# A list-scheduling planner with bank order, DMA lanes, held loads and repeated rounds, in a two-layer hybrid decoder trunk

## The chip, the cores and the metric

The kernel runs on one core of one Trainium2 chip. The metric is the device time of one execution in microseconds (us), as a median over runs. Five engines work in parallel, each through its own queue of instructions in a fixed order: PE (TensorE, matmuls; PEld is its loading of weights), DVE (VectorE), ACT (ScalarE), POOL (GpSimd) and SP (SyncE, which here only issues DMAs). ACT and POOL issue DMAs as well.

## The reference

A trunk of two pre-norm residual layers over 256 tokens of width 1024 in float32. Each layer makes one projection of the normalised stream, feeds three causal token mixers from it, gates, projects and sums them, and projects once more:

```python
for layer in range(DEPTH):
    h = rms_norm(x, norm_w[layer])
    proj = jnp.einsum('bsd,de->bse', h, w_in[layer])
    ...
    y_a = mamba2_branch(a_xbc, a_z, a_dt, conv_w[layer], ...)
    y_b = sliding_window_branch(b_q, b_k, b_v, b_z, sinks[layer], cos, sin)
    y_c = forgetting_attention_branch(c_q, c_k, c_v, c_f, c_z, f_bias[layer])
    branch = jnp.einsum('bsiw,iwd->bsid', jnp.stack([y_a, y_b, y_c], axis=2), w_proj[layer])
    g = jax.nn.sigmoid(gates.reshape(b, s, N_BRANCH, d) + gate_bias[layer])
    x = x + jnp.einsum('bsd,de->bse', jnp.sum(g * branch, axis=2), w_out[layer])
return rms_norm(x, final_norm_w)
```

The first mixer is a Mamba-2 scan in chunks of 128 tokens (4 groups of 4 heads), the second attention over a window of 128 with 16 query heads, 4 key heads and a learned sink per head, the third attention with a cumulative forgetting bias. Each has a SiLU gate of its own.

## The kernel before, in words

All weights stream from HBM once, in tiles of 512 KB (`raw`, six buffers), issued by SP. Float32 products are made of three reduced ones: ACT rounds a weight tile to `hi` (fp32r), DVE takes the rest as `lo`, and PE adds hi x high, hi x low and lo x high of the activations. The 256 tokens are two row blocks of 128. Products go to PSUM in two groups of banks: `mm` (three, for the dense products) and `mx` (five, for scores, transposes and scans). Activations live in tiles named by size (`L8`, `L4`, `L2`, `L1`).

The program is not written in the order in which it runs. The functions of `hybrid_trunk` (line 473) call a Recorder, which notes every operation with the tiles it reads and writes; `access` (line 235) finds from these what each operation depends on, by the elements it touches. The order on PE is the source's order, in which small generators (a quad of attention heads, a group of the scan) come up between the dense products after delays in us, the constants `D_...`. `D_CUM` is the delay of the cumulative sum of the log forget gates (`decay_logits`, line 1188).

The order of all other engines is made by a planner. `order_of` (line 267) gives every PE operation a nominal time, works back through the dependences to a due time for every other operation (`deadlines`, 306), and then runs the recorded program through a model (`run`, 322): at each step the engine that can begin first takes the operation with the earliest due time, unless one that is due sooner would be made late by more than `SLIP`. A DMA's landing is modelled with one `wire` that all queues share. The result feeds the next round, four in all; the last one is emitted (`emit`, 455, the emitting line 468, under which the profile lists every instruction).

The places that matter below: `attn_quad` and `swa_quad` (1008, 1161), which make a quad of four heads' scores in four `mx` banks, first narrow matmuls for one token block and then wide ones for the next, take masked maxima on DVE (`nm`, which starts from the negated sink `nsink`), exponentials on ACT (`pp`) and transpose these on PE; `ssd_group` (1277), the scan; `out_end` (1627), which adds the residual to the last projection, squares and sums it, multiplies it by the final norm's weight and by the row's factor `rs`, and stores it; and `load_final` (1683), a broadcast load of `final_norm_w` on ACT's queue.

Before, a load that depends on nothing is planned as soon as its buffer is free and the queue's turn comes.

Of the kernel before, what the change touches and what calls it, by code (L numbers as in the profile page):

```python
# [2 lines left out]

# [46 lines left out]
ENG = mybir.EngineType  # L50
ENGINES = ("tensor", "vector", "scalar", "gpsimd", "sync")
FIRST_WRITES = ("out", "accum_out")
SLIP, OPENING = 0.05, 16.0


class Buf:

    def __init__(self, tag, shape, dtype, space):
        self.tag, self.shape, self.dtype, self.space = tag, list(shape), dtype, space
        self.on_p = space != "dram"  # L60
        free = shape[1:] if self.on_p else shape
        self.n = int(np.prod(free)) if len(free) else 1
        self.ap = None
        self.turn = None
        self.users, self.open, self.last = [], 0, 0.0
# [70 lines left out]
class Op:  # L136

    def __init__(self, i, engine, name, args, kw):
        self.i, self.engine, self.name, self.args, self.kw = i, engine, name, args, kw
        self.ins = self  # L140
        self.deps, self.behind, self.after, self.bufs = set(), set(), [], []
        views = [("out" if k == 0 else "", a) for k, a in enumerate(args)] + list(kw.items())
        views = [(k, a) for k, a in views if isinstance(a, View)]
        self.writes = [a for k, a in views if k in FIRST_WRITES]
        self.reads = [a for k, a in views if k not in FIRST_WRITES]
        if name == "copy_predicated" or kw.get("accum_op") is not None:
            self.reads += self.writes
        sizes = [a.free_size() for _, a in views] or [1]
        self.cap = 1e9
# [48 lines left out]
class Recorder:  # L198
# [36 lines left out]
    def access(self, op, v, writes):  # L235
        b = v.buf
        if not b.users and b not in op.bufs:
            b.turn = self.turns[b.tag] = self.turns.get(b.tag, -1) + 1
            self.bufs.append(b)
            op.bufs.append(b)  # L240
        elif b not in op.bufs:
            op.behind.add(b.users[0].i)
        b.users.append(op)
        q = slice(v.p[0] // 32, (v.p[1] + 31) // 32) if b.on_p else slice(0, 1)
        e = np.unique(v.fx)
        deps = np.unique(b.writer[q][:, e])
        op.deps.update(int(d) for d in deps if d >= 0)
        if not writes:
            if op.engine == "tensor":
                b.pe_reader[q, e] = op.i  # L250
            else:
                mask = np.zeros(b.n, bool)
                mask[e] = True
                b.readers.append((op, q, mask))
            return
        op.deps.update(int(d) for d in np.unique(b.pe_reader[q][:, e]) if d >= 0)
        for r, rq, mask in b.readers:
            if r is not op and rq.start < q.stop and q.start < rq.stop and mask[e].any():
                op.deps.add(r.i)
        b.writer[q, e] = op.i  # L260
# [3 lines left out]
    return op.land if op.dma else op.end + op.lag  # L264


def order_of(rec, bufs_of, rounds=4, verbose=False):
# [12 lines left out]
    before = {}  # L280
    for tag, bs in by_tag.items():
        n = bufs_of[tag]
        for a, b in zip(bs, bs[n:]):
            before[id(b)] = a
    t = 0.0
    for op in ops:
        if op.engine == "tensor":
            op.nominal = t
            t += op.busy
    end = t  # L290
    for _ in range(rounds):
        deadlines(ops, before, end)
        end, before = run(ops, by_tag, bufs_of)
        t = 0.0
        for op in ops:
            if op.engine == "tensor":
                t = op.start if op.start < OPENING else t
                op.nominal = t
                t += op.busy
        end = t + 8.0  # L300
        if verbose:
            print("end", round(end, 1))
    return sorted(ops, key=lambda op: (op.start, op.i))


def deadlines(ops, before, end):
    for op in ops:
        op.late = op.nominal + op.busy if op.engine == "tensor" else min(op.cap, end + 50.0)
    for op in reversed(ops):
        op.due = min(op.nominal, op.late - op.busy) if op.engine == "tensor" else op.late - op.busy  # L310
        for d in op.deps:
            o = ops[d]
            o.late = min(o.late, op.due - (o.away if o.dma else o.lag))
        for b in op.bufs:
            a = before.get(id(b))
            if a is not None:
                for o in a.users:
                    if o.i < op.i:
                        o.late = min(o.late, op.due - (o.away if o.dma else o.lag))


def run(ops, by_tag, bufs_of):
# [8 lines left out]
    waits = {tag: set(range(len(bs))) for tag, bs in by_tag.items()}  # L331
    soon = {e: sorted((op for op in ops if op.engine == e), key=lambda op: (op.due, op.i)) for e in ENGINES[1:]}
    before = {}
# [4 lines left out]
    wire = 0.0  # L338
    done = 0
    forced = False  # L340

# [10 lines left out]

    def when(op):
        t = op.ready
        for b in op.bufs:
            p = place_time(b)
            if p is None:
                return None
            skipped = sum(x < b.turn for x in waits[b.tag])
# [31 lines left out]
    while done < len(ops):  # L391
        best = None
        for e in ENGINES:
            if e == "tensor":
                if at == len(pe) or pe[at].left:
                    continue
                c = [(when(pe[at]), pe[at])]
            else:
                c = [(when(op), op) for op in queues[e]]
            c = [(max(r, free[e]), op) for r, op in c if r is not None]  # L400
# [3 lines left out]
            r, op = min(((r, op) for r, op in c if r <= t0 + 1e-9), key=lambda x: (x[1].due, x[1].i))  # L404
            if e != "tensor" and not forced and t0 > OPENING:
                until = guarded(e, t0, op)
                if until is not None:
                    c = [(r, op) for r, op in c if r + op.busy <= until + 0.02 or op.due < until]
# [3 lines left out]
                    r, op = min(((r, op) for r, op in c if r <= t0 + 1e-9), key=lambda x: (x[1].due, x[1].i))  # L412
            if best is None or r < best[0]:
                best = (r, e, op)
        forced = best is None
        if forced:
            continue
# [1 line left out]
        op.start, op.end = r, r + op.busy  # L419
        free[e] = op.end  # L420
        if op.dma:
            if op.start < OPENING:
                wire = max(wire, op.end + 0.8) + op.kb / 330
                op.land = max(wire + 1.0, op.end + 2.2)
            else:
                wire = max(wire, op.end + 0.8) + op.kb * (1.5 if op.kb < 270 else 1.0) / 270
                op.land = max(wire + 2.0, op.end + (4.3 if e == "gpsimd" else 2.8))
        for b in op.bufs:
            _, i = place_time(b)
            old = places[b.tag][i][1]  # L430
            if old is not None:
                before[id(b)] = old
            places[b.tag][i] = (None, b)
            waits[b.tag].discard(b.turn)
            b.slot = i
        if e == "tensor":
            at += 1
# [8 lines left out]
        for o, whole in op.after:  # L446
            o.left -= 1
            o.ready = max(o.ready, f if whole else op.start + 0.01)
            if not o.left and o.engine != "tensor":
                queues[o.engine].append(o)  # L450
        done += 1
# [1566 lines left out]
```

## Time and profile before

| | |
|---|---|
| median of 3 runs | 820.79 us (820.53 to 822.17) |
| profiled execution, its own time | 822.48 us |
| its span in the trace | 820.8 us |
| mean granted TensorE clock | 0.996 |
| instructions | 14838 |
| HBM read over the span | 154.71 MB, 191 GB/s |

Times in the views are us from the start of the span. A row of the timeline gives the start, the duration of the group, the engine, the line, the operation, the tile written and those read, the shape, the count, and in brackets the idle time of the engine before it with what ended that. Since every instruction has line 468, tiles tell the places apart: `mx<-L,qt` are scores of a sliding-window quad, `mm<-hi,L` and `mm<-L,hi` dense products. The durations of neighbours overlap, as engines begin an instruction before the last has drained.

### The profile page before, as it was taken

What the parts mean: (1) busy time and instruction counts of PE and PEld (TensorE: products, weight loads), DVE (VectorE), ACT (ScalarE), POOL (GpSimd) and SP (SyncE); (2) the same over time, 40 slices, a digit from 0 to 9 for tenths busy, and PEclk for the clock granted to TensorE, in tenths of its full rate; (3) what the DMA queues carried; (4) which work ended last, traced back from release to release, by engine and by line L of the source; (5) the groups of instructions that cost most, each with busy time, mean ns of one, the idle gap of its engine ahead of it and who ended that gap; (6) DMA issues with size and microseconds to landing.
All of it is one profiled execution on the core that took longest, in us unless ns stands there. A gap on an engine that the chain in (4) does not pass through costs nothing.

```text
span 820.8 us, 14838 instructions
## 1 busy us (share of the span) xinstructions
PE 803.6 (98%) x5160; PEld 714.4 (87%) x5160; DVE 684.9 (83%) x1416; ACT 542.4 (66%) x1146; POOL 165.7 (20%) x236
## 2 busy tenths in 40 slices
PE   7999999999999999999999999999999999999996
PEld 6998888988988988888998898888888888888896
DVE  5968898998889997796685889989888989959874
ACT  5876788775666795544465568777757668755461
POOL 4245312130303300020001731222212120001100
PEclk9999999999999999999999999999999999999999
DMA  9899897797836575666668967789987465556731
GB/s 267 265 282 221 212 245 189 220 269 222 224 113 221 173 216 168 203 222 208 210 226 259 246 157 222 194 216 255 242 255 200 151 197 162 177 198 217 231 103 52
DMA packets 138826, 170.43 MB, mean 208 GB/s; under 512 B 9352, under 2 KB 106464, under 8 KB 138752
## 3 DMA queue, kind: packets, MB, share of 16 engines
q1 hardware_dynamic: 114960, 140.53, 56.5%
q0 software_dynamic: 13328, 13.29, 9.9%
q10 hardware_dynamic: 10464, 15.67, 6.0%
q8 instruction: 41, 0.67, 0.3%
q14 instruction: 33, 0.27, 0.1%
HBM read 154.71 MB, written 2.16 MB: 191 GB/s over the span
## 4 chain that ended last, share of the span: by engine, by line
PE 95%; DVE 2%; DMA 1%; issue 0%; SPq 0%; ACT 0%; DVEq 0%; ACTq 0%
PE mm L468 83%; PE mx L468 12%; DMA raw<-in_w_in_dram 1%; DVE L L468 1%; SPq L468 0%; ACT hi L468 0%; DVE lo L468 0%; DVE pp L468 0%; ACT L L468 0%; DVE sm L468 0%; DVE rs L468 0%; DVEq L468 0%; DVE nm L468 0%; ACTq L468 0%; DVE ss L468 0%
## 5 line engine op out<-in xcount | busy, mean ns | idle before, releaser
L468 DVE TENSOR_TENSOR lo<-raw,hi 128x1024 fp32r<-128x1024 f32 (+2 forms) x292 | 329.7, 1144 | 56.3 <-ACT hi L468 46.7
L468 PE MATMUL mm<-L,hi 128*128 128x512 f32 x1056 | 355.1, 388 | 0.0
L468 ACT ACTIVATE hi<-raw 128x1024 fp32r<-128x1024 f32 (+2 forms) x292 | 281.3, 975 | 99.2 <-PE mm L468 75.4
L468 PE MATMUL mm<-hi,L 128*128 128x512 f32 (+2 forms) x1168 | 303.4, 349 | 1.5 <-ACT L L468 1.2
L468 PE MATMUL mm<-L,lo 128*128 128x256 f32 x1056 | 267.1, 273 | 0.0
L468 PEld LDWEIGHTS mm<-hi,L 128*128 128x128 f32 x1168 | 206.0, 190 | 24.7 <-issue 1.8
L468 PEld LDWEIGHTS mm<-L,hi 128*128 128x128 f32 x1056 | 195.5, 190 | 26.6 <-issue 3.0
L468 PEld LDWEIGHTS mm<-L,lo 128*128 128x128 f32 x1056 | 202.8, 192 | 5.5
L468 PE MATMUL mm<-lo,L 128*128 128x512 f32 (+2 forms) x584 | 201.2, 347 | 0.0
L468 ACT ACTIVATE L<-L 128x256 f32<-128x256 f32 (+2 forms) x184 | 89.4, 505 | 68.7 <-DVE L L468 62.5
L468 PEld LDWEIGHTS mm<-lo,L 128*128 128x128 f32 x584 | 110.3, 190 | 10.7
L468 POOL DMA_DIRECT2D L<-L x80 | 65.2, 859 | 206.8 <-ACT L L468 166.6
L468 ACT ACTIVATE L<-mm 128x256 f32<-128x256 f32 (+2 forms) x202 | 67.9, 373 | 44.3 <-PE mm L468 37.4
L468 ACT ACTIVATE pp<-pp,nm 128x128 f32<-128x128 f32 (+1 forms) x96 | 40.8, 427 | 26.9 <-DVE nm L468 26.7
L468 DVE TENSOR_TENSOR L<-mm,L 128x256 f32<-128x256 f32 (+1 forms) x70 | 37.1, 532 | 22.5 <-PE mm L468 22.1
L468 DVE SCALAR_TENSOR_TENSOR L<-L,vec,L 128x255 f32<-128x255 f32 (+3 forms) x112 | 51.2, 476 | 1.3 <-ACT L L468 0.9
L468 POOL TENSOR_SCALAR_AFFINE_SELECT bias<-bias 128x128 f32<-128x128 f32 x64 | 32.6, 558 | 74.4 <-DMA bias<-cumd 74.0
L468 DVE SCALAR_TENSOR_TENSOR L<-L,L 128x256 f32<-128x256 f32 (+1 forms) x94 | 44.2, 479 | 1.0 <-ACT L L468 0.8
L468 ACT ACTIVATE L<-mx 128x512 f32<-128x512 f32 (+3 forms) x48 | 26.5, 572 | 13.8 <-PE mx L468 13.8
L468 DVE TENSOR_TENSOR L<-L,L 128x512 fp32r<-128x512 f32 (+2 forms) x56 | 32.6, 595 | 0.3
L468 POOL TENSOR_TENSOR sm<-sm,mhalf 128x8 f32<-128x8 f32 (+2 forms) x5 | 6.1, 1222 | 129.3 <-DVE sm L468 129.3
L468 POOL TENSOR_TENSOR L<-L,L 128x512 f32<-128x512 f32 (+1 forms) x12 | 15.6, 1330 | 77.4 <-DVE L L468 77.4
(139 smaller groups left out, 678.2 us busy)
## 6 DMA issues: line engine op xcount, KB each, us to landing
raw<-in_w_in_dram SPq DMA_DIRECT2D x191, 512.0 KB, 5.0
raw<-in_w_proj_dram SPq DMA_DIRECT2D x48, 512.0 KB, 5.1
L<-L POOLq DMA_DIRECT2D x72, 128.0 KB, 5.1
raw<-in_w_out_dram SPq DMA_DIRECT2D x16, 512.0 KB, 5.2
bias<-cumd ACTq DMA_DIRECT2D x16, 256.0 KB, 4.6
L<-cumd ACTq DMA_DIRECT2D x8, 512.0 KB, 6.6
L<-in_gate_bias_dram ACTq DMA_DIRECT2D x12, 256.0 KB, 4.1
qt<-L POOLq DMA_DIRECT2D x16, 128.0 KB, 5.2
```

Source lines behind the costliest of these rows:

```text
L468: getattr(getattr(nc, op.engine), op.name)(*map(real, op.args), **{k: real(v) for k, v in op.kw.items()})
```

## The change

Five edits, all in the planner but the last.

1. The Recorder's `access` keeps a table `latest` per PSUM buffer: an access by one engine depends on the latest accesses of every other engine to the same buffer, whatever elements they touch. Accesses of different engines to a bank thus stand in the source's order.
2. The model of DMAs has eight lanes for the queues of SP and ACT and eight for POOL's: a DMA begins when the eighth last before it has landed. Each queue has a wire, and they slow each other.
3. A load that depends on nothing, is no weight tile and is due after 10 us is held behind the PE operation that nominally begins `LEAD` = 20 us before its due time.
4. Seven rounds in place of four; from the third on a PE operation that came late is given an earlier due time in the next, and the round with the earliest end is kept. `SLIP` is 0.3 instead of 0.05.
5. `D_CUM` is 20 instead of 17.

```diff
-D_GN1, D_GN2, D_CUM, D_H, D_M = 8.0, 3.0, 17.0, (4.8, 6.4), 5.0
+D_GN1, D_GN2, D_CUM, D_H, D_M = 8.0, 3.0, 20.0, (4.8, 6.4), 5.0
...
-SLIP, OPENING = 0.05, 16.0
+SLIP, OPENING, LEAD = 0.3, 16.0, 20.0
...
         b.users.append(op)
+        if b.space == "psum":
+            for e, o in b.latest.items():
+                if e != op.engine:
+                    op.deps.update(o)
+            if op.engine == "tensor":
+                b.latest[op.engine] = [op.i]
+            else:
+                b.latest.setdefault(op.engine, []).append(op.i)
...
+            for op in ops:
+                if op.dma and not op.deps and op.bufs and op.bufs[0].tag != "raw" and op.due > 10.0:
+                    x = pe[bisect.bisect(at, op.due - LEAD) - 1]
+                    op.behind.append(x.i)
+                    op.held = True
+                    x.after.append((op, False))
+        end, before = run(ops, by_tag, bufs_of)
+        t = late = last = 0.0
+        for op in pe:
+            gap, last = op.start - last, op.end
+            if op.start > OPENING and gap > 0.03:
+                late += gap
+                if n > 1:
+                    op.early += gap + 0.3
...
+        if best is None or end < best[0]:
+            best = (end, [(op.start, op.end) for op in ops], [b.slot for b in rec.bufs])
...
     def when(op):
         t = op.ready
+        if op.dma:
+            t = max(t, lanes[op.engine == "gpsimd"][-8])
...
-                wire = max(wire, op.end + 0.8) + op.kb * (1.5 if op.kb < 270 else 1.0) / 270
-                op.land = max(wire + 2.0, op.end + (4.3 if e == "gpsimd" else 2.8))
+            early = op.start < OPENING
+            now, c = op.end + 0.8, op.kb / (330 if early else 300)
+            left = max(wire[q] - now for q in wire if q != e)
+            wire[e] = max(wire[e], now) + c + max(0.0, min(c, left))
```

The order on PE is the same but for the cumulative sums, on SP the same. In a row below, a name is the tile's tag with its buffer and its number, and the brackets name the engines or DMA lanes whose semaphores the instruction waits for.

PE, the wide score matmuls of layer 0's first quad (`mx` 10 to 13 are its four banks, `qt` the queries), before:

```order
L468 MATMUL mx_3_12_946<-L8_5_5_759,qt_0_0_844 128x256
L468 MATMUL mx_0_13_948<-L8_5_5_759,qt_0_0_844 128x256
L468 MATMUL mx_2_10_942<-L8_5_5_759,qt_0_0_844 128x256 [waits DVE_49]
L468 MATMUL mx_4_11_944<-L8_5_5_759,qt_0_0_844 128x256 [waits DVE_49]
L468 MATMUL mx_3_12_946<-L8_5_5_759,qt_0_0_844 128x256 [waits DVE_49]
L468 MATMUL mx_0_13_948<-L8_5_5_759,qt_0_0_844 128x256
```

The same place now:

```order
L511 MATMUL mx_3_12_922<-L8_5_5_702,qt_0_0_775 128x256
L511 MATMUL mx_0_13_924<-L8_5_5_702,qt_0_0_775 128x256
L511 MATMUL mx_2_10_918<-L8_5_5_702,qt_0_0_775 128x256
L511 MATMUL mx_4_11_920<-L8_5_5_702,qt_0_0_775 128x256
L511 MATMUL mx_3_12_922<-L8_5_5_702,qt_0_0_775 128x256
L511 MATMUL mx_0_13_924<-L8_5_5_702,qt_0_0_775 128x256
```

The second four matmuls no longer wait for DVE: the instructions and their order are unchanged.

ACT in the opening (`hi` and `raw` 0 to 3 are the first weight tiles, `L2` 4 and 10 the two halves of a gate's bias), before:

```order
L468 DMA L2_0_4_79<-in_gate_bias_dram 128x512
L468 ACT_TABLE_LOAD
L468 ACTIVATE tab_0_0_67<-tab_0_0_67 128x1 [waits DVE_49]
L468 ACTIVATE L2_1_0_111,ss_0_0_112<-L8_0_0_69 128x512 [waits DMAHW1_49]
L468 ACTIVATE L2_2_1_131,ss_0_0_112<-L8_0_0_69 128x512 [waits DMAHW3_49]
L468 ACTIVATE L8_2_2_141<-L8_1_1_125 128x512 [waits DVE_49]
L468 DMA L2_3_10_149<-in_gate_bias_dram 128x512 [waits DMAHW4_49]
L468 ACTIVATE hi_0_0_159<-raw_0_0_83 128x512
L468 ACTIVATE L8_2_2_141<-L8_1_1_125 128x512 [waits DVE_49]
L468 ACTIVATE hi_0_0_159<-raw_0_0_83 128x512 [waits DMAHW5_49]
```

and now:

```order
L511 ACTIVATE hi_1_1_175<-raw_1_1_100 128x512 [waits DMAHW5_49]
L511 ACTIVATE hi_1_1_175<-raw_1_1_100 128x512
L511 ACTIVATE L2_2_2_192,ss_0_0_120<-L8_0_0_69 128x512 [waits DMAHW6_49]
L511 ACTIVATE L2_3_3_202,ss_0_0_120<-L8_0_0_69 128x512
L511 ACTIVATE L8_2_2_142<-L8_1_1_129 128x512 [waits DVE_49]
L511 ACTIVATE hi_2_2_219<-raw_2_2_112 128x512 [waits DMAHW0_49]
L511 ACTIVATE L8_2_2_142<-L8_1_1_129 128x512 [waits DVE_49]
L511 ACTIVATE hi_2_2_219<-raw_2_2_112 128x512
L511 ACTIVATE hi_3_3_239<-raw_3_3_126 128x512 [waits DMAHW1_49]
L511 ACTIVATE hi_3_3_239<-raw_3_3_126 128x512
L511 DMA L2_4_4_257<-in_gate_bias_dram 128x512 [waits DMAHW7_49]
L511 ACTIVATE hi_4_4_264<-raw_4_4_131 128x1024 [waits DMAHW2_49]
```

The first bias load has gone behind the rounding of weight tile 3 and the second to the stretch around 131 us; the per-head loads on POOL's queue go behind PE operations in the same way.

ACT in the tail (`L8` 35 holds the residual of both row blocks, `ss` their sums of squares, `rs` the rows' factors; `L4` 27 is the final norm's weight), before:

```order
L468 ACTIVATE L2_1_104_9621,ss_3_3_9622<-L8_5_35_9615 128x256 [waits DVE_49]
L468 ACTIVATE L2_8_105_9628,ss_0_4_9629<-L8_5_35_9615 128x256 [waits DVE_49,Pool_49]
L468 ACTIVATE L2_5_107_9660,ss_3_3_9622<-L8_5_35_9615 128x512 [waits DVE_49]
L468 ACTIVATE sm_2_14_9694<-sm_1_13_9669 128x1 [waits DVE_49]
L468 ACTIVATE L8_5_35_9615<-L8_5_35_9615,rs_1_5_9704 128x384 [waits DVE_49]
L468 DMA out_0_dram<-L8_5_35_9615 128x384 [waits Activation_49]
L468 ACTIVATE L2_2_110_9734,ss_0_4_9629<-L8_5_35_9615 128x512 [waits DVE_49]
L468 ACTIVATE sm_5_18_9760<-sm_0_17_9743 128x1 [waits DVE_49]
L468 ACTIVATE L8_5_35_9615<-L8_5_35_9615,rs_2_6_9766 128x384 [waits DVE_49]
L468 DMA out_0_dram<-L8_5_35_9615 128x384 [waits Activation_49]
```

and now:

```order
L511 ACTIVATE L2_2_107_9655,ss_3_3_9619<-L8_5_35_9612 128x512 [waits DVE_49]
L511 ACT_TABLE_LOAD
L511 ACTIVATE sm_2_14_9687<-sm_1_13_9664 128x1 [waits DVE_49]
L511 ACTIVATE L2_3_110_9723,ss_0_4_9626<-L8_5_35_9612 128x512 [waits DVE_49]
L511 DMA L4_1_27_9743<-in_final_norm_w_dram 128x1024
L511 ACTIVATE sm_5_18_9749<-sm_0_17_9732 128x1 [waits DVE_49]
L511 ACTIVATE tab_0_0_67<-ones_0_0_90 128x1
L511 ACTIVATE L8_5_35_9612<-L8_5_35_9612,rs_1_5_9697 128x384 [waits DVE_49]
L511 ACTIVATE L8_5_35_9612<-L8_5_35_9612,rs_2_6_9755 128x384 [waits DVE_49]
L511 DMA out_0_dram<-L8_5_35_9612 128x384 [waits Activation_49] x2
```

The load of the norm's weight has moved here from some 140 rows further up (there behind gate bias 88), and the two stores stand together at the end. DVE at the same place (`mm` 225 and 226 are the last two products of the second row block), before:

```order
L468 TENSOR_TENSOR L8_5_35_9615<-mm_0_225_9681,L2_0_109_9380 128x512 [waits DMAHW5_49,PE_49]
L468 TENSOR_REDUCE sm_0_17_9743<-ss_0_4_9629 128x1 [waits Activation_49]
L468 SCALAR_TENSOR_TENSOR L8_5_35_9615<-L8_5_35_9615,L4_2_27_8186 128x512 [waits DVE_49]
L468 TENSOR_SCALAR sm_0_17_9743<-sm_0_17_9743 128x1 [waits DVE_49]
L468 TENSOR_TENSOR L8_5_35_9615<-mm_2_226_9723,L1_9_351_8855 128x256 [waits PE_49]
L468 ISA L2_3_111_9756,ss_0_4_9629<-L8_5_35_9615 128x256 [waits DVE_49]
L468 ISA ss_0_4_9629 128x1
L468 SCALAR_TENSOR_TENSOR sm_0_17_9743<-ss_0_4_9629,sm_0_17_9743 128x1 [waits DVE_49]
L468 SCALAR_TENSOR_TENSOR L8_5_35_9615<-L8_5_35_9615,L4_2_27_8186 128x256
L468 RECIPROCAL sm_2_19_9762<-sm_5_18_9760 128x1 [waits Activation_49]
L468 SCALAR_TENSOR_TENSOR sm_1_20_9764<-sm_2_19_9762,sm_0_17_9743 128x1 [waits DVE_49]
L468 SCALAR_TENSOR_TENSOR rs_2_6_9766<-sm_1_20_9764,sm_2_19_9762 128x1 [waits DVE_49]
```

and now:

```order
L511 TENSOR_TENSOR L8_5_35_9612<-mm_2_226_9712,L1_10_351_8852 128x256 [waits PE_49]
L511 ISA L2_4_111_9746,ss_0_4_9626<-L8_5_35_9612 128x256 [waits DVE_49]
L511 ISA ss_0_4_9626 128x1
L511 SCALAR_TENSOR_TENSOR sm_0_17_9732<-ss_0_4_9626,sm_0_17_9732 128x1 [waits DVE_49]
L511 RECIPROCAL sm_2_19_9751<-sm_5_18_9749 128x1 [waits Activation_49]
L511 SCALAR_TENSOR_TENSOR sm_1_20_9753<-sm_2_19_9751,sm_0_17_9732 128x1 [waits DVE_49]
L511 SCALAR_TENSOR_TENSOR rs_2_6_9755<-sm_1_20_9753,sm_2_19_9751 128x1 [waits DVE_49]
L511 SCALAR_TENSOR_TENSOR L8_5_35_9612<-L8_5_35_9612,L4_1_27_9743 128x512 [waits DMAHW2_49]
L511 SCALAR_TENSOR_TENSOR L8_5_35_9612<-L8_5_35_9612,L4_1_27_9743 128x512
L511 SCALAR_TENSOR_TENSOR L8_5_35_9612<-L8_5_35_9612,L4_1_27_9743 128x256 x4
L511 TENSOR_SCALAR L8_5_35_9612<-L8_5_35_9612,rs_1_5_9697 128x640 [waits DVE_49]
L511 TENSOR_SCALAR L8_5_35_9612<-L8_5_35_9612,rs_2_6_9755 128x640 [waits DVE_49]
```

All multiplications by the norm's weight stand behind the second row block's factor, with a wait for the load's lane on the first.

More of the change, by code (lines that the diff above doesn't have):

```diff
@@ L64, in __init__ @@
         self.turn = None
-        self.users, self.open, self.last = [], 0, 0.0
+        self.users, self.open, self.last, self.latest = [], 0, 0.0, {}
         self.writer = np.full((4, self.n), -1, np.int32)
@@ L284, in order_of @@
             before[id(b)] = a
+    pe = [op for op in ops if op.engine == "tensor"]
     t = 0.0
-    for op in ops:
-        if op.engine == "tensor":
+    for op in pe:
+        op.nominal, op.early = t, 0.0
+        t += op.busy
+    end, best = t, None
+    for n in range(rounds):
+        deadlines(ops, before, end)
+        if not n:
+            at = [op.nominal for op in pe]
+            for op in ops:
[6 more added lines that the diff above has]
+        t = late = last = 0.0
+        for op in pe:
+            gap, last = op.start - last, op.end
[3 more added lines that the diff above has]
+                    op.early += gap + 0.3
+            t = op.start if op.start < OPENING else t
             op.nominal = t
             t += op.busy
[L290 to L299, printed above, removed]
+        if best is None or end < best[0]:
+            best = (end, [(op.start, op.end) for op in ops], [b.slot for b in rec.bufs])
+        if verbose:
+            print("round", n, "end", round(end, 2), "late", round(late, 2))
         end = t + 8.0
-        if verbose:
-            print("end", round(end, 1))
+    for op, (op.start, op.end) in zip(ops, best[1]):
+        pass
+    for b, b.slot in zip(rec.bufs, best[2]):
+        pass
     return sorted(ops, key=lambda op: (op.start, op.i))
@@ L309, in deadlines @@
     for op in reversed(ops):
-        op.due = min(op.nominal, op.late - op.busy) if op.engine == "tensor" else op.late - op.busy
+        op.due = op.late - op.busy
+        if op.engine == "tensor":
+            op.due = min(op.nominal, op.due) - op.early
         for d in op.deps:
@@ L330, in run @@
     places = {tag: [(0.0, None)] * bufs_of[tag] for tag in by_tag}
-    waits = {tag: set(range(len(bs))) for tag, bs in by_tag.items()}
+    waits = {tag: list(range(len(bs))) for tag, bs in by_tag.items()}
     soon = {e: sorted((op for op in ops if op.engine == e), key=lambda op: (op.due, op.i)) for e in ENGINES[1:]}
+    for op in ops:
+        if op.held:
+            waits[op.bufs[0].tag].remove(op.bufs[0].turn)
     before = {}
@@ L358, in when @@
                 return None
-            skipped = sum(x < b.turn for x in waits[b.tag])
+            skipped = bisect.bisect_left(waits[b.tag], b.turn)
             if skipped and sum(old is None or not old.open for _, old in places[b.tag]) <= skipped:
@@ L414, in run @@
                 best = (r, e, op)
+        if best is None and forced:
+            raise RuntimeError("no operation can begin")
         forced = best is None
@@ L421, in run @@
         if op.dma:
[L422 to L425, printed above, removed]
-                wire = max(wire, op.end + 0.8) + op.kb * (1.5 if op.kb < 270 else 1.0) / 270
-                op.land = max(wire + 2.0, op.end + (4.3 if e == "gpsimd" else 2.8))
+            early = op.start < OPENING
+            now, c = op.end + 0.8, op.kb / (330 if early else 300)
+            left = max(wire[q] - now for q in wire if q != e)
+            wire[e] = max(wire[e], now) + c + max(0.0, min(c, left))
+            for q in wire:
+                if q != e and wire[q] > now:
+                    wire[q] += min(c, wire[q] - now)
+            op.land = max(wire[e] + (1.0 if early else 2.5),
+                          op.end + (2.2 if early else 4.5 if e == "gpsimd" else 3.2))
+            lanes[e == "gpsimd"].append(op.land)
         for b in op.bufs:
@@ L433, in run @@
             places[b.tag][i] = (None, b)
-            waits[b.tag].discard(b.turn)
+            waits[b.tag].remove(b.turn)
             b.slot = i
@@ L448, in run @@
             o.ready = max(o.ready, f if whole else op.start + 0.01)
+            if not o.left and o.held:
+                bisect.insort(waits[o.bufs[0].tag], o.bufs[0].turn)
             if not o.left and o.engine != "tensor":
```

8 lines of the change are left out of this document (5 added, 3 removed).

## Prediction

> **What bounds the kernel now.** The first part of the page, its busy times, comes first:
>
> ```profile
> PE 803.6 (98%) x5160; PEld 714.4 (87%) x5160; DVE 684.9 (83%) x1416; ACT 542.4 (66%) x1146; POOL 165.7 (20%) x236
> ```
>
> TensorE is busy for 803.6 of 820.8 us, so only 17.2 us are to be had from waiting. The table by stretches says where they lie (columns: stretch, its length, busy time and instructions of PE, PEld, DVE, ACT and POOL, granted clock, DMA share, GB/s):
>
> ```profile
> 0.00:20.00 20.00, 15.36 (x89) 12.74 (x90) 10.64 (x19) 11.42 (x23) 9.59 (x28) 1.00 0.93 264
> 20.00:70.00 50.00, 50.00 (x324) 46.13 (x326) 40.08 (x62) 39.22 (x81) 21.62 (x30) 1.00 0.97 273
> 455.00:480.00 25.00, 23.44 (x152) 20.38 (x151) 18.81 (x40) 14.08 (x33) 14.24 (x19) 0.93 0.92 208
> 800.00:821.00 21.00, 14.47 (x91) 13.15 (x89) 9.55 (x29) 3.73 (x12) 0.00 (x0) 0.91 0.14 51
> ```
>
> 4.6 us are missing in the opening, 6.5 at the end, where TensorE has no more work, and 6.1 between. At 455 to 480 the clock dips too: 7% of 25 us, 1.75 us. The waits of PE name the releasers (us in total, times, longest):
>
> ```profile
> PE mx L468 <- DVE nm L468: 3.7, 6, 1.6
> PE mx L468 <- DVE L L468: 1.3, 3, 0.6
> PE mm L468 <- ACT L L468: 1.2, 1, 1.2
> PE mm L468 <- DVE L L468: 1.1, 2, 0.6
> ```
>
> The first row is the sliding-window quads, the second and fourth mostly the scans, the third the opening. Everywhere else PE runs without a gap, so time goes down only by what goes from these rows, and goes up by what the new order puts before a matmul or behind the last one.
>
> **The quads: 7.6 us less.** A quad is 24 score matmuls, then eight wide ones that write, for the second half, banks which DVE is still reading for the first half's maxima (nm). From PE's timeline stand the narrow part of quad 1, then the wide parts of the quads that wait (of three alike, at 142.82, 498.62 and 545.19, the first and the last), and a quad without a wait:
>
> ```profile
> 69.80 1.16 PE L468 MATMUL mx<-L,qt 32*128 32x128 f32 x24
> 71.39 1.25 PE L468 MATMUL mx<-L,qt 32*128 32x256 f32 x8 [0.43 <-DVE nm L468]
> ...
> 96.52 0.71 PE L468 MATMUL mx<-L,qt 32*128 32x256 f32 x8 [0.43 <-DVE nm L468]
> ...
> 142.82 0.98 PE L468 MATMUL mx<-L,qt 32*128 32x256 f32 x8 [0.43 <-DVE nm L468]
> ...
> 471.87 1.57 PE L468 MATMUL mx<-L,qt 32*128 32x256 f32 x8 [1.56 <-DVE nm L468]
> ...
> 545.19 0.98 PE L468 MATMUL mx<-L,qt 32*128 32x256 f32 x8 [0.43 <-DVE nm L468]
> ```
> ```profile
> 119.65 1.59 PE L468 MATMUL mx<-L,qt 32*128 32x128 f32 x32
> ```
>
> Each waiting quad takes 1.16 + gap + wide part; less the 1.59 of the free one that is 1.25, 0.71, 0.98, 2.70, 0.98 and 0.98: 7.6 us. In the new order the wide matmuls carry no wait for DVE, since DVE's reads now follow the second write. All 7.6 lie on PE, hence on the path. The clock's dip stands around the 1.56 us gap; about 0.45 of its 1.75 us is in that quad's 2.70 already, so 1.3 more go with it if the gap is the cause, nothing if not. I take 1.3.
>
> **The scans: 2.3 us less.** In each layer the last matmuls of two sums wait for DVE, which reads the same bank early:
>
> ```profile
> 233.33 0.32 PE L468 MATMUL mm<-L,L 128*64 128x128 f32 x1 [0.57 <-DVE L L468]
> ...
> 235.45 0.43 PE L468 MATMUL mx<-L,L 128*64 128x128 f32 x2 [0.58 <-DVE L L468]
> ```
>
> That is 1.15 us a layer, 2.3 in two (the two rows of waits on DVE L, 2.4 in all, leave no room for more). D_CUM moves three cumulative-sum matmuls a layer behind the next weight tile; they take the same time there, and what hangs on them (a round trip through DRAM) is not needed for over 10 us: nothing.
>
> **The opening: 2.0 us less.** Both gate-bias loads of layer 0 and the small per-head and conv loads leave the first 18 us. What the queues there carry (packets, MB, share of the 16 engines in 0 to 20 us), and PE's waits there for weights:
>
> ```profile
> q1 hardware_dynamic: 4025, 4.62, 70.8%
> q0 software_dynamic: 416, 0.13, 11.6%
> q10 hardware_dynamic: 304, 0.53, 10.5%
> ```
> ```profile
> 8.76 0.49 PE L468 MATMUL mx<-hi,L 128*128 128x256 f32 x2 [0.38 <-ACT hi L468]
> 9.80 0.94 PE L468 MATMUL mx<-hi,L 128*128 128x256 f32 x6 [0.55 <-ACT hi L468]
> ...
> 17.43 1.30 PE L468 MATMUL mm<-hi,L 128*128 128x256 f32 x6 [1.25 <-ACT L L468]
> ```
>
> 0.66 of 5.28 MB go, 12.5% of 20 us: the weights come up to 2.5 us sooner. But PE's own order, its filler matmuls included, stays; only its gaps can close. From the first weight on these are 0.38 + 0.55 + 1.25 and four small ones, about 2.5. I take 2.0, between 0 and 2.5, nearer the top because the moved bytes alone would allow it.
>
> **New waits: 0.9 us more.** The sinks' load of layer 0 now stands behind a PE operation, so that the first quad's nsink comes on POOL behind two rope transfers, and DVE's nm behind lo 27. By hand, from the before's times of these rows, its probabilities are ready at about the instant at which PE transposes them: 0 to 1.2, say 0.5, and as little again (0.4) for one weight split (lo 139, at 419 us) that gets several operations ahead of it.
>
> **The tail: 4.6 us more.** The load of final_norm_w was issued at 660.8 us. It now stands on ACT behind the last 512-wide square, and DVE's six multiplications by it, which were spread between the last evictions, stand behind everything but the two row scalings. ACT's and DVE's end before:
>
> ```profile
> 812.55 0.63 ACT L468 ACTIVATE L<-L 128x512 f32<-128x512 f32 x1 [3.29 <-DVE L L468]
> 813.09 0.19 ACT L468 ACTIVATION_READ_ACCUMULATOR L<-L 128x1 f32 x1
> ```
> ```profile
> 813.38 0.68 DVE L468 SCALAR_TENSOR_TENSOR L<-L,L 128x512 f32<-128x512 f32 x1
> ...
> 815.51 0.42 DVE L468 SCALAR_TENSOR_TENSOR L<-L,L 128x256 f32<-128x256 f32 x1
> ...
> 816.50 0.55 DVE L468 TENSOR_SCALAR L<-L,rs 128x640 f32<-128x640 f32 x1
> ```
> ```profile
> L<-in_final_norm_w_dram ACTq DMA_DIRECT2D x1, 512.0 KB, 5.5
> bias<-cumd ACTq DMA_DIRECT2D x1, 256.0 KB, 3.3
> ```
> ```profile
> out_dram<-L SPq DMA_DIRECT2D x2, 320.0 KB, 3.2
> ```
>
> In the before's clock the load is issued at 813.3. It took 5.5 us among other traffic; half its size took 3.3, and the other 256 KB at the opening's 264 GB/s are 1.0 more. With nothing else on the queues I take 4.1, with 3.3 and 5.5 as ends: it lands at 817.4, 0.9 after the instant (816.5) at which the last row scaling began. Then six multiplications, 2 x 0.60 + 4 x 0.35 without their overlap, 2.6; then the other row block's scaling, 0.5, before the last one. So the last scaling begins 4.0 us later. Both blocks' results, 1 MB, then leave at once where one left before, whose 320 KB took 3.2 us: 0.6 more (0 to 1.0). Sum 4.6, ends 3.2 and 6.6. No other work hides it, since PE has ended at 814.5.
>
> The Trainium skill, page DMA: Bandwidth & Descriptors, section "Rules for kernel authors", speaks against this edit: issue a DMA early and wait for it late, so that its fixed cost overlaps. The same page ("Anatomy of one DMA") fits 2.0 us plus the bytes at 436 GB/s, by which the load would take an estimated 3.2 us and the tail 3.7 instead of 4.6. The 3.3 and 5.5 above lie over that, and they decide.
>
> **Sum.** 7.6 + 1.3 + 2.3 + 2.0 = 13.2 less, 0.9 + 4.6 = 5.5 more: 7.7 us less than the profiled execution's 822.48, 814.8. The median of the runs shown, 820.79, is 1.7 below that execution: **813.1 us**.
>
> **Rivals.**
> - The tail is hidden: the multiplications fit in DVE's idle time, or the load comes earlier than its place suggests. Against it: its row has only the two scalings behind it, and in the stretch 800 to 821 nothing else remains. 813.1 - 4.6 = 808.5; chance 0.13.
> - The opening gives nothing, because the moved loads return where the DMA engines are 0.97 busy (20 to 70 us) and weights come late there, and the tail costs its upper end: 813.1 + 2.0 + 2.0 = 817.1. For it: that row's 0.97. Against it: PE has no gap in those 50 us, at 273 GB/s. Chance 0.16.
> - Only part of the waits goes, the scans' and the dip staying, with both of these: 817.1 + 3.6 = 820.7, no change; chance 0.07.
> - Slower: the wait goes from the bank to the transposes of the probabilities. DVE reads a quad's scores only after the whole quad, ACT's exponentials stand behind weight splits, and PE meets the transposes too early. Before, the first quad's probabilities were ready 7.9 us ahead of use (75.25 to 83.16); in the new order that reserve is nearly gone there, so it can be.
>
> ```profile
> 74.57 0.68 DVE L468 TENSOR_TENSOR pp<-pp,rsum 128x512 f32<-128x512 f32 x1
> ```
> ```profile
> 83.16 0.60 PE L468 MATMUL mx<-ident,pp 128*128 128x128 f32 x4
> ```
> This rival decides above 1.3 us in each of the eight quads ((822.4 - 813.1 + 0.9) / 8); at 2 us each the time is 813.1 + 16 - 0.9 = 828.2. Against it: at the other quads the rows ahead of the exponentials did not grow so. Chance 0.09.
>
> **How the numbers follow.** The forecast's case has 0.55. Its own bounds: all gains full and the tail cheap (3.2), 809.7; opening nil and tail 6.6, 817.1. The range 809.0 to 818.5 leaves out the fully hidden tail, the no-change and the slower case, and half the chance of those near its edges. A measurement of this kernel tells 0.2%, 1.6 us, from no change: faster 0.84 (0.55 + 0.13 + 0.16), same 0.07, slower 0.09.
>
> **What would show it.** Right: the row PE mx <- DVE nm is gone, a quad takes 1.59 everywhere, the clock is 1.00 at 455 to 480, PE's gap of 1.25 us ahead of 17.43 closes and the row that it stands in comes some 2 us sooner, and in the tail DVE waits for final_norm_w's DMA and ends some 7 us after the last matmul (2.6 before). Wrong: a new wait of PE for pp or hi in the quads, gaps in 20 to 70, or a tail of the old length.

## The result, and the profile after

The changed kernel takes 809.37 us (median of 4 runs, 809.29 to 809.45) where the kernel before took 821.48 beside it (820.53 to 822.72): a ratio of 0.9852, with a 95% interval of 0.9835 to 0.9869. That is 12.1 us faster, and 3.7 under the forecast of 813.1. The profiled execution took 809.29, its span is 807.6, 13.2 less than before.

The page's busy times of the kernel after, then its table by stretches (columns as in the prediction):

```profile
PE 795.6 (99%) x5160; PEld 711.8 (88%) x5160; DVE 683.3 (85%) x1416; ACT 542.3 (67%) x1146; POOL 172.0 (21%) x236
```
```profile
0.00:20.00 20.00, 17.68 (x124) 16.59 (x125) 13.69 (x28) 14.22 (x26) 5.85 (x19) 1.00 0.92 309
20.00:70.00 50.00, 50.00 (x333) 45.57 (x332) 40.67 (x61) 37.40 (x78) 18.88 (x25) 1.00 0.99 265
...
455.00:480.00 25.00, 25.00 (x188) 22.89 (x187) 21.09 (x51) 17.98 (x53) 17.00 (x26) 1.00 0.96 216
785.00:808.00 23.00, 13.30 (x85) 12.13 (x83) 8.60 (x28) 4.35 (x10) 0.00 (x0) 0.90 0.19 69
```

From 20 us to its end PE is full but for 0.3 us, the clock is 1.00 at 455 to 480 where it was 0.93, and in the opening PE has begun 124 matmuls by 20 us where it had begun 89. All waits of PE that are left:

```profile
PE mx L511 <- POOL ident L511: 1.4, 1, 1.4
PE mx L511 <- DMA L<-in_x_dram: 0.7, 1, 0.7
PE mx L511 <- DVE es L511: 0.3, 1, 0.3
```

The waits for `nm`, for the scans' reads and for ACT in the opening are gone; one is new, for `es` (the sinks' term of the row sums), at the transposes of layer 0's first quad. The scores of that quad, and of layer 1's, stand as one row each, as wide as the quad that never waited:

```profile
65.88 1.59 PE L511 MATMUL mx<-L,qt 32*128 32x128 f32 x32
```
```profile
460.72 1.59 PE L511 MATMUL mx<-L,qt 32*128 32x128 f32 x32
```

Laying PE's matmuls of the two traces side by side, in their common order, shows where the lead over before grows. Each row names a place, and gives the start of the matmul just after it in both traces, the lead there, and what the place itself adds to the lead:

| place | before | after | lead | gained here |
|---|---|---|---|---|
| weight tile 3's first `lo` matmul | 18.79 | 14.87 | 3.92 | 3.9 |
| after quad 1, layer 0 | 72.57 | 67.41 | 5.16 | 1.25 |
| at its transposes | 83.16 | 78.48 | 4.68 | -0.5 |
| after quad 2 | 97.16 | 91.80 | 5.36 | 0.72 |
| after quad 4 | 143.73 | 137.39 | 6.34 | 0.98 |
| after the two scans' waits, layer 0 | 235.81 | 227.66 | 8.15 | 1.8 |
| after quad 1, layer 1 | 473.37 | 462.24 | 11.13 | 2.70 |
| 2.7 us later (the dip of the clock) | 476.09 | 463.66 | 12.43 | 1.30 |
| after quad 2 | 499.53 | 486.12 | 13.41 | 0.98 |
| after quad 4 | 546.10 | 531.71 | 14.39 | 0.98 |
| after the scans' waits, layer 1 | 638.18 | 621.98 | 16.19 | 1.8 |

Between these places only a transpose at 393 us adds more, 0.3. At the end PE leads by 16.2 us, and the span by 13.2: the tail gives 3.0 back. It was 6.3 from the last matmul to the span's end and is 9.3. Its rows on DVE and ACT after:

```profile
800.14 0.16 DVE L511 SCALAR_TENSOR_TENSOR rs<-sm,sm 128x1 f32<-128x1 f32 x1
800.22 2.63 DVE L511 SCALAR_TENSOR_TENSOR L<-L,L 128x512 f32<-128x512 f32 x6
802.76 1.01 DVE L511 TENSOR_SCALAR L<-L,rs 128x640 f32<-128x640 f32 x2
```
```profile
796.38 0.63 ACT L511 ACTIVATE L<-L 128x512 f32<-128x512 f32 x1 [4.58 <-DVE L L511]
796.39 0.34 ACTq L511 DMA_DIRECT2D L<-in_final_norm_w_dram  x1
```
```profile
L<-in_final_norm_w_dram ACTq DMA_DIRECT2D x1, 512.0 KB, 3.7
```

The load is issued while ACT still squares (796.39, not after it), takes 3.7 us and lands at 800.1, as the last row factor comes (800.14). So its flight is hidden, and DVE goes from the factor to the multiplications without idle time. What is paid is the multiplications (2.63 us) that now stand in one row behind the factor, and the first row block's scaling.

### The profile page after: what moved, and what is told of

It reads as the page before. It is cut to its first block, busy times and chain, and to the rows that moved or that the text cites. A ratio compares the mean times of both kernels' runs of the same rounds, so it can differ in the third digit from the quotient of the medians.

```text
span 807.6 us, 14854 instructions
## 1 busy us (share of the span) xinstructions
PE 795.6 (99%) x5160; PEld 711.8 (88%) x5160; DVE 683.3 (85%) x1416; ACT 542.3 (67%) x1146; POOL 172.0 (21%) x236
## 4 chain that ended last, share of the span: by engine, by line
PE 96%; POOL 1%; DVE 1%; issue 1%; DMA 0%; ACT 0%; DVEq 0%; POOLq 0%; ACTq 0%
PE mm L511 83%; PE mx L511 13%; POOL L L511 1%; DVE L L511 1%; DMA L<-in_x_dram 0%; POOL hb L511 0%; POOL qt L511 0%; ACT L L511 0%; DVE pp L511 0%; DVE nm L511 0%; DVE es L511 0%; DVE sm L511 0%; DVEq L2057 0%; POOL nsink L511 0%; ACT sm L511 0%
## 5 line engine op out<-in xcount | busy, mean ns | idle before, releaser
L511 POOL DMA_DIRECT2D L<-L x80 | 68.0, 900 | 184.2 <-ACT L L511 176.9
L511 POOL TENSOR_SCALAR_AFFINE_SELECT bias<-bias 128x128 f32<-128x128 f32 x64 | 39.0, 707 | 84.3 <-DMA bias<-cumd 84.0
L511 DVE SCALAR_TENSOR_TENSOR L<-L,vec,L 128x254 f32<-128x254 f32 (+3 forms) x112 | 51.9, 478 | 2.2 <-ACT L L511 2.0
L511 ACT ACTIVATE L<-L,vec 128x256 f32<-128x256 f32 (+1 forms) x48 | 26.8, 566 | 14.2 <-DMA L<-L 14.1
```

Of the source, the lines that this page charges most:

```text
L511: getattr(getattr(nc, op.engine), op.name)(*map(real, op.args), **{k: real(v) for k, v in op.kw.items()})
```

## The experiments

Every run's ratio is against runs of the kernel before on the same chip, whose median there was 822.4 to 822.6. In what follows "lead" is again the lead of PE over the kernel before in the aligned traces.

**Final norm's load free.** The held loads without the one of 512 KB on ACT:

```diff
-                if op.dma and not op.deps and op.bufs and op.bufs[0].tag != "raw" and op.due > 10.0:
+                if op.dma and not op.deps and op.bufs and op.bufs[0].tag != "raw" and op.due > 10.0 and not (op.kb > 500 and op.engine == "scalar"):
```

> The changed kernel, but the load of the final norm's weight alone is not held. Main theory: its late place costs the tail 3.0 us (all six multiplications behind the last row factor), so the time is 809.4 - 3.0 = 806.4, and the stretch from the last matmul to the end is 6.3 us again instead of 9.3. Rival: the tail is set by the last stores and the row factors, and the moved load meets busy queues near 660 us: 809.4 or a little more.

Measured 806.03 (ratio 0.9794, 0.9775 to 0.9814), span 804.3. The multiplications stand between the last evictions again, and the last scaling comes one row behind the last factor:

```profile
799.00 0.42 DVE L511 SCALAR_TENSOR_TENSOR L<-L,L 128x256 f32<-128x256 f32 x1
...
799.80 0.16 DVE L511 SCALAR_TENSOR_TENSOR rs<-sm,sm 128x1 f32<-128x1 f32 x1
800.00 0.56 DVE L511 TENSOR_SCALAR L<-L,rs 128x640 f32<-128x640 f32 x1
```

From the last row factor's start to the last scaling's start it is 0.20 us; in the changed kernel it is 3.1 (800.14 to about 803.2). The late load was a loss of the change, and this version beats both kernels.

**No bank order.** The changed kernel without edit 1:

```diff
-        if b.space == "psum":
-            for e, o in b.latest.items():
-                if e != op.engine:
-                    op.deps.update(o)
-            ...
```

> The changed kernel without the bank order in access; loads held, lanes, rounds and D_CUM as changed. Main theory: the waits of PE on the quads' and scans' banks come back, 7.8 + 3.6 us, and the clock's dip of 1.3 with them: about 822. Rival: the repeated rounds and the larger slip already take half of those waits, and about 815 is seen.

Measured 815.89 (0.9912, 0.9888 to 0.9935): the main theory fails by half. PE's waits of this run:

```profile
PE mx L503 <- DVE nm L503: 1.3, 3, 0.4
PE mx L503 <- DVE L L503: 1.2, 2, 0.6
PE mm L503 <- DVE L L503: 1.2, 2, 0.6
```

The scans' four waits are back, and three of the quads'. Three quads stay free: the first of both layers, so that the gap of 1.56 and the dip stay away, and layer 1's second (why that one does was not traced). Bank order is then worth 815.89 - 809.37 = 6.5 on top of the rest: in the alignment three quads (1.0 each) and the scans (3.6) make 6.5. In this run DVE reads the first quad's first half only after it has waited for the negated sink, some 6 us after PE's second write (67.6):

```profile
73.92 0.35 DVE L503 CUSTOM_DVE_ANT_0 pp<-mx,wmask,nsink 128x128 f32<-128x128 f32 x1 [0.51 <-POOL nsink L503]
```

**Bank order alone**, in the kernel before:

```diff
...
         b.users.append(op)
+        if b.space == "psum":
+            for e, o in b.latest.items():
+                if e != op.engine:
+                    op.deps.update(o)
+            ...
```

> The kernel before with the bank order in access and nothing else of the change. Main theory: quads, scans and the dip give 12.7 us alone, 821.5 - 12.7 = 808.8, the opening and the tail as before. Rival: without the new model of the DMAs and the repeated rounds the later reads make new waits elsewhere, and half is lost: about 815.

Measured 811.66 (0.9859, 0.9833 to 0.9885). Alone it frees all the banks' waits: the lead grows by 12.5 from 20.8 us on, where 12.7 was expected. But the new plan's opening is 2.4 longer, by this wait, with a dip behind it:

```profile
18.24 1.52 PE L476 MATMUL mm<-hi,L 128*128 128x256 f32 x8 [2.54 <-ACT L L476]
```
```profile
20.00:25.00 5.00, 5.00 (x32) 5.00 (x32) 4.33 (x10) 3.76 (x6) 3.31 (x5) 0.67 0.96 344
```

**Nothing held.** The changed kernel without edit 3:

```diff
-                if op.dma and not op.deps and op.bufs and op.bufs[0].tag != "raw" and op.due > 10.0:
+                if False:
```

> The changed kernel with no load held. Main theory: the opening goes back to the old one (+3.9) and the tail as well (-3.0): 810.3, with the gate biases in the first 10 us. Rival: the opening is shorter because of the new order of ACT and the row sums, not of the loads: 806.4.

Measured 822.54 (0.9998, 0.9988 to 1.0007): neither theory. PE falls 10 us behind the kernel before in the first 33 us. The chain of waits shows what was not foreseen:

```profile
3.84 5.43 DMA hb<-in_sinks_dram
9.27 0.09 issue
9.36 0.44 POOL nsink L511
...
10.92 4.99 DMA hb<-in_d_skip_dram
...
16.92 4.91 DMA hb<-in_a_log_dram
21.85 0.21 ACT nega L511
22.07 0.53 ACT hi L511
```

The small per-head loads run one behind the other on POOL, each some 5 us in flight, and the planner has put the ACT operation that uses the last of them (`nega`) ahead of weight tile 2's rounding. ACT's queue, and with it every weight, waits for a load of 8 KB.

**ACT's loads free.** The loads on POOL held, those on ACT not:

```diff
-                if op.dma and not op.deps and op.bufs and op.bufs[0].tag != "raw" and op.due > 10.0:
+                if op.dma and not op.deps and op.bufs and op.bufs[0].tag != "raw" and op.due > 10.0 and op.engine != "scalar":
```

> As the run with the final norm's load free, but all of ACT's loads free (the gate biases, 0.53 MB of them in the opening, the loads of the residual, the final norm); POOL's small loads still held. Main theory: the opening is a matter of bytes ahead of the weights, and 0.53 MB at 264 to 310 GB/s cost 1.7 to 2.0 us: 806.0 + 1.8 = 807.8, with the wait in front of weight tile 2 back. Rival: the small loads on POOL, each some 5 us in flight, made the old opening long: 806.0 to 806.5.

Measured 823.19 (1.0005, 0.9991 to 1.0019). At weight tile 3 the lead is 1.64 against 4.11 in the run with only the final norm free, so the opening costs 2.5, with a wait of 2.00 us for x at its second transposes. But 5.1 more are lost from 20 to 37 us, and a wait for probabilities in layer 1 adds its own, so the total says nothing about bytes, and the opening little: each new set of loads is a new plan for all engines.

```profile
488.15 1.00 PE L511 MATMUL mx<-ident,pp 128*128 128x128 f32 x4 [3.69 <-DVE pp L511]
```

From 20 to 37 the chain of waits runs through evictions on ACT that stand ahead of weight roundings and wait for PE. Why the planner's rounds kept that plan was not traced.

**Sinks sooner.** The final norm free, and the per-head loads held 35 instead of 20 us ahead:

```diff
-                    x = pe[bisect.bisect(at, op.due - LEAD) - 1]
+                    x = pe[bisect.bisect(at, op.due - LEAD - (15.0 if op.bufs[0].tag == "hb" else 0.0)) - 1]
```

> As the run with the final norm's load free, with the per-head loads held 35 instead of 20 us ahead of use. Main theory: the one new wait of PE (for es, 0.2 to 0.3 at the first quad's transposes, 0.35 to 0.5 in the alignment) goes: 805.6. Rival: it is set by ACT's queue of exponentials, not by the sinks: no change, 806.0.

Measured 805.66 (0.979, 0.9772 to 0.9809). The wait for `es` is gone from PE's waits, as the main theory has it. The time differs from the 806.03 of the run without it by less than the measurement tells.

**Four rounds.**

```diff
-def order_of(rec, bufs_of, rounds=7, verbose=False):
+def order_of(rec, bufs_of, rounds=4, verbose=False):
...
-                    op.early += gap + 0.3
+                    op.early += 0.0
```

(and `SLIP` 0.05.)

> The changed kernel with four rounds, no earlier due times for late PE operations and SLIP 0.05 as before. Main theory: with the banks in order and the loads held PE has hardly a wait left, and the rounds are worth little: 809.4, within 1. Rival: the repeated rounds removed new waits that the bank order makes: 812 or more, with waits of PE on lo or pp.

Measured 810.13 (0.9841, 0.982 to 0.9863): 0.8 slower than the changed kernel by the time, no slower by the ratio (0.9852 there). The rounds carry little, as the main theory has it.

**No bank order, sinks early.** As the run without bank order, with the per-head loads held 40 us longer ahead, so that the sinks are there before the quads (`op.due - LEAD - 40.0` for them):

> The changed kernel without the bank order, with the per-head loads held 60 us ahead of use, so that the sinks are there before each layer's first quad. Main theory: without bank order the first quads ran free only because the held sinks made DVE's reads late; now their waits return, 1.25 + 2.7 us and the clock's dip of 1.3: 815.9 + 5.2 = 821. Rival: the repeated rounds had removed them: 815.9.

Measured 818.92 (0.996, 0.9942 to 0.9977). All six quads wait again:

```profile
PE mx L503 <- DVE nm L503: 2.9, 6, 0.7
```

So in the run without bank order the first quads were free because the held sinks made DVE read their banks late, after PE's second write; the rounds had not freed them. Only 3.0 of the 5.2 come back (1.8 between the two profiled executions; this run's ten go from 817.7 to 823.2). Layer 1's first wait is now 0.48, not 1.56, and the clock at 455 to 480 is 1.00 in this run.

**Gate bias in front.** The run with the final norm free, its plan untouched; only the first gate bias load is issued first of all (`.start = 0.0` for it before the operations are sorted).

> The run with the final norm's load free, its order kept as planned, except that the first gate bias load (256 KB) is issued at the very front as before the change. Main theory: bytes ahead of the first weights cost their time on the wires, 0.26 MB at 264 to 310 GB/s: 806.0 + 0.9 = 806.9, all of it before 20 us. Rival: the opening's gain came from the new order of ACT and DVE, not from the bytes: 806.0.

Measured 807.94 (0.9819, 0.9787 to 0.9851), 1.9 more, but not by the way that the theory has it. Of the 2.1 us of lead that are lost, 1.86 are lost at the first transpose, which waits for the 4 KB of norm weights queued behind the 256 KB on ACT; by weight tile 3 only 0.2 more have been lost. Since PE begins that much later, weights that came up to 1.9 us later would hardly be seen: the run does not tell what the bytes alone cost.

```profile
PE mx L513 <- DMA L<-in_norm_w_dram: 1.8, 1, 1.8
```

**Small loads in front.** The same run, with the ten per-head loads of 8 KB issued in POOL's opening (`op.start = 3.0` for them):

> The run with the final norm's load free, its order kept as planned, except that the ten per-head loads (8 KB each, 80 KB) are issued in POOL's opening. Theory by bytes: 0.3 us at most, 806.0 to 806.3. Rival, by the share of engine time that POOL's queue had before (11.6% of 20 us): 2 us, 808. Either way the one wait for es at the first quad stays, since nsink keeps its place.

Measured 810.81 (0.9854, 0.9826 to 0.9882), 4.8 more; the lead at weight tile 3 is gone (18.82 against 18.79 before, 14.68 in the run without them). The queues of both runs in the first 20 us, with the small loads in front, and without:

```profile
q1 hardware_dynamic: 3888, 4.42, 67.7%
q0 software_dynamic: 320, 0.08, 21.0%
```
```profile
q1 hardware_dynamic: 4742, 5.99, 90.1%
```

80 KB hold 21% of the engines' time, and 1.57 MB fewer of x and the weights arrive by 20 us. The theory by bytes is wrong by a factor of more than ten. The theory by engine time had the wrong share: it took the 11.6% of the kernel before. By the 21% of this run it gives 4.2 us, and 4.1 of lead are lost by weight tile 3.

**D_CUM back at 17**, on the run with the final norm free:

> The run with the final norm's load free, with D_CUM 17 as before. Main theory: the sums' place costs or gives nothing but what the alignment shows around them (0.1 us a layer): 805.7 to 806.1. Rival: the earlier place collides with the banks' order there and PE waits on DVE: 807 or more.

Measured 805.87 (0.9795, 0.9768 to 0.9821): no difference.

**The old wire**, no lanes and one wire in the model, on the same run:

> The run with the final norm's load free, planned with the old model of one wire and no lanes. Main theory: the model of the DMAs moves rows but no wait of PE hangs on it: 806 to 806.8. Rival: without lanes ACT and POOL meet loads whose lane is still taken, and PE waits behind them: 809 or more.

Measured 805.76 (0.9793, 0.9767 to 0.982): no difference, and no wait for `es` in its trace. Of the change's edits the model of the DMAs and D_CUM thus are worth nothing that can be measured here, and the rounds no more than the 0.8 above, which the intervals do not tell from nothing.

## Why the prediction was right, and where it was off

The direction and the places held; four terms were mis-sized, all four on the cautious side.

| term | predicted | measured |
|---|---|---|
| quads | -7.6 | -7.6 |
| clock's dip | -1.3 | -1.3 |
| scans | -2.3 | -3.6 |
| opening | -2.0 | -3.9 |
| new waits | +0.9 | +0.5 |
| tail | +4.6 | +3.0 |
| a transpose at 393 us | 0 | -0.3 |
| sum | -7.7 | -13.2 |

The sum is off by 5.5, the forecast by only 3.7, and part of that is luck. The forecast took another 1.7 off to come from the profiled execution (822.48) to the median of three runs, and the medians of the kernel before in later sets, 821.5 to 822.6, lie nearer to that execution. From 822.48 the measured terms give 809.3, the measured time. By the prediction's own terms its best case is 810.3 (0.5 more in the opening, no new wait, 1.4 less in the tail), not the 809.7 that it states, and the tail's upper end is 6.4, not 6.6. The measured 809.37 lies below that best case: the range held by its margin down to 809.0.

- **Quads.** Right in size and cause: bank order alone frees all six. One thing was unforeseen: the first quad of each layer is freed twice, by bank order and by the held sinks. The runs without bank order show it, one with late sinks (those two quads free) and one with early (all six wait).
- **The dip.** It left with the 1.56 us gap, as taken. That a gap of this length brings it is not shown: waits of 1.61 and 1.62 in other runs left the clock at 1.00.
- **Scans.** The step that failed is pricing a wait by the idle time in brackets (0.57 and 0.58). The alignment gives 1.8 a layer for these 1.15, that is 0.90 for each wait. Before, it was 4.57 us from the first of these matmuls (231.24) to the first behind them (235.81); after, it is 2.77, in rows without a break:

```profile
224.89 1.53 PE L511 MATMUL mm<-L,L 128*64 128x128 f32 x24
226.25 1.48 PE L511 MATMUL mx<-L,L 128*64 128x128 f32 x24
227.66 1.58 PE L511 MATMUL mx<-qt 64*128 64x128 f32 x16
```

One such matmul alone lasts 0.27 us, and 24 of them 1.53: without a wait each begins before the ones ahead have drained. A wait costs its idle time and that overlap, here 0.33 more. The quads were priced from start to end, and came out right.
- **Opening.** The step that only PE's gaps can close, about 2.5 in all, failed in size: it is the sum of bracketed idle times again. The cause was taken as 0.66 MB ahead of the weights, and that was wrong in two ways. The first gate bias did not leave the first 18 us. It stands behind two roundings of tile 3 in ACT's queue, but was issued before either of them ran:

```profile
13.44 0.36 ACTq L511 DMA_DIRECT2D L<-in_gate_bias_dram  x1
13.66 2.34 ACT L511 ACTIVATE hi<-raw 128x512 fp32r<-128x512 f32 x3
```

And bytes are the wrong measure for the small loads: 80 KB in front of an unchanged plan take all of the 3.9 back. The engines' time fits better. In the rows that the prediction shows, POOL's queue (q0) and ACT's (q10) hold 11.6% and 10.5% of it in the first 20 us. After, POOL's queue carries nothing there and ACT's holds 3.6%; the 18.5% less are 3.7 us of 20, an estimate. How the 3.9 are split between the small loads and the gate biases is not shown: the 256 KB in front cost 1.9, but through a queue.

```profile
q1 hardware_dynamic: 4698, 5.91, 88.5%
q10 hardware_dynamic: 158, 0.26, 3.6%
```

- **New waits.** The first quad's came as reckoned (0.5 for 0.5); that for weight split 139 did not come.
- **Tail.** The mechanism is shown by the run that leaves the load free, 3.3 faster. Mis-sized were the issue (796.39, with the square, not after it, 0.7 sooner than reckoned) and the flight (3.7 for 4.1), so that the load costs nothing by itself, and the stores of both blocks together, for which 0.6 was taken: from the last scaling's start to the end it is 4.3 us before and 4.4 after. The multiplications (2.5) and the other block's scaling (0.5) are as reckoned. The sign named for it came in part: DVE ends 5.5 us after the last matmul, not some 7, and loses no time to the load. The Trainium skill, page DMA: Bandwidth & Descriptors ("Rules for kernel authors"), says to issue a DMA early and wait for it late, so that its fixed cost overlaps. Here the load is issued late and its 3.7 us of flight are hidden even so, behind the row factors; it is the order of the work behind the load that costs. The prediction's estimate of 3.2 us rests on a fit that the same page of the Trainium skill ("Anatomy of one DMA") gives for DMAs issued from GpSimd; this load is on ACT's queue, and the measured 3.7 decides.
- **The rivals.** The tail hidden (808.5) came nearer to the time than the forecast, yet it is not what happened: the tail lost 3.0, and the opening and the scans gave 3.2 more than reckoned. PE met the transposes too early only once, for 0.3 us.

## What to carry to other kernels

Price a wait on PE from start to start, against a row of the same work that did not wait: the idle time shown leaves out the overlap that is lost, 0.33 us for each wait in the scans here. Where a planner lets an engine read a bank early, nothing is gained if PE writes the same bank next; the ordering rule for banks was worth more here than a better model of costs. Loads that nobody needs yet should leave the opening when they are many and small: price them by their share of the DMA engines' time, not by their bytes. But a rule that holds every load back must leave out those at the program's end, where the work behind the load has no cover.

## What the runs showed of the hardware

- Ten loads of 8 KB in the first 20 us held 21% of the DMA engines' time. All DMAs together moved 225 GB/s there, and 314 in the run without them; the kernel took 4.8 us more.
- The granted clock dipped behind waits of PE of 1.56 us (0.77 in 470 to 475), 2.54 (0.67 in 20 to 25, the run with bank order alone), 3.13 (0.81 in 20 to 25, nothing held) and 3.69 (0.83 in 490 to 495, ACT's loads free). Each dip is a stretch of 3.4 us at 0.50, as here in the kernel before. Waits of 1.61 (nothing held, at 416.68) and 1.62 (ACT's loads free, at 412.38) left the clock at 1.00, so the length of the wait alone does not decide. The Trainium skill, page TensorE: Matmul & The Clock Gate (Part 1), puts the gate at an idle window of about 3.4 us; three of the four waits are shorter, so here the measurement decides.

```profile
472.66:476.07 3.41, 3.41 (x13) 2.43 (x11) 2.55 (x13) 1.04 (x6) 0.00 (x0) 0.50 0.68 176
```

- In its first 8 us PE runs at about half its later pace, though the clock column reads 1.00 for 0 to 20 us: the same eight transposes of x take 1.97 us for the first row block and 1.04 for the second.

```profile
4.12 1.97 PE L511 MATMUL mx<-ident,L 128*128 128x128 f32 x8 [0.73 <-DMA L<-in_x_dram]
...
10.21 1.04 PE L511 MATMUL mx<-ident,L 128*128 128x128 f32 x8
```

- A DMA issued on ACT did not wait for the activations that stand ahead of it: the final norm's load began 0.01 us after the start of the square (796.39), the first gate bias 0.2 us before the start of the rounding ahead of it (13.44).
